# The second feed-forward's up products as seven products of halves

## The chip, the cores and the metric
The kernel runs on one core of one Trainium2 chip. The metric is the device time of one execution in microseconds; for the kernel before it is 1956.56 us, the median of 3 runs (1956.21 to 1960.05).

## What is computed
A diffusion backbone of two layers over 512 latent tokens (and 256 context tokens, which only the first layer still updates). Each layer has an attention part and a feed-forward part. The change concerns the feed-forward of the second layer, on the 512 latent tokens alone:

```python
def conv_ffn(h, w_up, conv_w, conv_b, w_down):
    u = h @ w_up                      # 512 x 1024 by 1024 x 5632
    n_tok = u.shape[1]
    pad = CONV_W // 2                 # CONV_W = 3
    up = jnp.pad(u, ((0, 0), (pad, pad), (0, 0)))
    u = sum(up[:, i:i + n_tok] * conv_w[i] for i in range(CONV_W)) + conv_b
    a, g = jnp.split(u, 2, axis=-1)   # 2816 columns each
    return (jax.nn.silu(g) * a) @ w_down

x = x + g2 * conv_ffn(modulate(x, g_ffn[l], sh2, s2), w_up[l], conv_w[l], conv_b[l], w_down[l])
```

All of it is float32.

## The kernel before
Activations are kept transposed: eight blocks of 128 features lie on the 128 partitions, tokens along the free dimension. TensorE multiplies in a reduced format (fp32r), so each operand is split in a high part (a rounded copy) and a low part (the rest), and a product is three matmuls: high by high, high by low, low by high (`mm3`, L254 to L257; the matmul itself is L252). `split` (L226) makes the two parts: the high part on ACT (L229) or POOL (L231), the low part on DVE (L237) or POOL (L239), as a subtraction of two SBUF tiles.

The normed tokens are 16 tiles: eight high (`self.hh`) and eight low (`self.hl`), in the group of buffers named E in the second layer; the running state x is eight tiles of the group F, and the feed-forward's hidden h goes to F too. `out_norm` computes the norm in two halves of 256 tokens: the last attention products and the residual update (L1335), squares on ACT (L530), sums by matmuls with a column of ones (L539), the root on POOL (L267, L269), its transpose on PE (the rows `pt<-ident,rr`, L261), scale and shift (L556, L557), and the split (high on POOL, low on DVE and POOL by turns).

`ffn` (L1465 on) goes over 22 pairs of up tiles: pair i is the 128 hidden columns i of the half a and the same of the half g (tile 22 + i). For a pair, `up_w` loads two weight tiles of 128 x 1024 (raw, buffers `fr`) and splits them (buffers `fu`; the second of pair 1 in `fd`), ACT the high and DVE the low part. `up_mm` makes eight steps of three matmuls with 512 columns for each tile into a PSUM tile `s`: 48 per pair. Pair 0 is done in two halves of 256 tokens, so that its first half needs only the first half of the norm. `up_tile` does the convolution: a scaled copy from PSUM on ACT (L1422) and taps on DVE that read PSUM (`tap`, L1440: two of 504 columns, two of 7). Then come silu on ACT (L1513), the product on DVE (L1514) and the split of h (high on POOL, low on DVE).

Pairs go in chunks of two. The down products of a chunk (`accumulate`: eight output blocks, 2 x 3 matmuls of 512 each, 48 per chunk, into PSUM tiles o, acc and pt, each followed by a residual update on DVE, L1335) run one chunk later, after the second pair's up products. Their weights come by `down_w` (buffers `fr` and `fd`). The last pair is finished in two halves by `last_part`.

The instruction streams of each engine are ordered by a scheduler that simulates the program on a timeline and takes what it holds to be ready; the order is then fixed. What can be taken early depends on buffers: the pool of the second layer's mixing part (its tiles u, s, raw among them) is closed before the pools of the feed-forward are opened, and where a new pool takes memory of an old one, its tiles wait for the old tiles' last readers. The pool for `fu` lies on the other side of the memory than that for `fr` and `fd`.

## Time and profile before

| | before |
|---|---|
| median of 3 runs | 1956.56 us |
| profiled execution | 1957.14 us |
| its span on the core | 1955.4 us |
| PE busy | 1857.2 us (95%) |
| DVE busy | 1189.5 us (61%) |
| ACT busy | 797.5 us (41%) |
| POOL busy | 748.4 us (38%) |
| second feed-forward | about 1581 us to the end of the span |

PE stands for TensorE's matmuls, PEld for its weight loads (which run beside them), DVE for VectorE, ACT for ScalarE, POOL for GpSimd. Busy time counts what an instruction takes on its engine. A row of a group gives line, engine, operation, output and inputs, shapes and count, then the busy time, the mean in ns, and the idle time before with what ended it. A row of a timeline gives start and duration in us, and how many instructions it sums. PEclk is the share of full clock that was granted to TensorE.

### The profile page before, as it was taken

To read this page: it belongs to the slowest core of one execution; us is meant where nothing else is said; L and a number is where in the kernel's file an instruction comes from. 1 tells how busy PE (TensorE), PEld (TensorE's weight loads), DVE (VectorE), ACT (ScalarE), POOL (GpSimd) and SP (SyncE) were. 2 spreads that over 40 slices of the span, in tenths; PEclk is the share of its full clock that TensorE was granted. 3 is DMA by queue.
4 is the path that set the end of the run, shared out by engine and by line. 5 is a ranking of instruction groups with operands and counts; after the bars stand their busy time and mean duration, and the time that the engine had idled before them with its cause. 6 is when DMAs were issued, how large, how long until landed. Compare 5 with 4: busy or idle time off the path is not lost.

```text
span 1955.4 us, 32438 instructions
## 1 busy us (share of the span) xinstructions
PE 1857.2 (95%) x12513; PEld 1613.9 (83%) x12513; DVE 1189.5 (61%) x2132; ACT 797.5 (41%) x1549; POOL 748.4 (38%) x1013
## 2 busy tenths in 40 slices
PE   5999999989999999999999999998989999999999
PEld 3778888878898788888888898887977788888888
DVE  5344566365467677865566575457356467666665
ACT  4336546375444222222222254655356453323332
POOL 4555363460045545668761047544362030000000
PEclk9999999899999999999999999999999999999999
DMA  9852333421213434254442124233431313333332
GB/s 315 293 166 53 99 82 84 130 94 48 79 42 113 112 98 137 80 171 138 122 134 69 60 71 113 53 96 100 107 105 58 91 50 104 93 96 93 97 97 76
DMA packets 177081, 206.19 MB, mean 105 GB/s; under 512 B 10848, under 2 KB 142784, under 8 KB 174880
## 3 DMA queue, kind: packets, MB, share of 16 engines
q1 hardware_dynamic: 175872, 201.96, 34.9%
q0 software_dynamic: 1056, 2.16, 0.4%
...
## 4 chain that ended last, share of the span: by engine, by line
PE 77%; DVE 7%; DMA 5%; POOL 5%; ACT 3%; issue 2%; SPq 1%; POOLq 0%; ACTq 0%; DVEq 0%
PE s L252 32%; PE acc L252 18%; PE pt L252 10%; PE o L252 6%; PE pt L261 5%; PE o L862 4%; DMA wr<-in_w_in 1%; DMA wr<-in_w_out 1%; POOL rr L269 1%; DVE fu L237 1%; POOL wh L239 1%; DVE m L816 1%; PE s L539 1%; DVE p L1440 1%; ACT p L819 1%
## 5 line engine op out<-in xcount | busy, mean ns | idle before, releaser
L252 PE MATMUL s<-F,fu 128*128 128x256 f32 (+1 forms) x2064 | 374.0, 336 | 0.3 <-DVE p L1440 0.3
L252 PEld LDWEIGHTS s<-F,fu 128*128 128x128 f32 x2064 | 314.1, 189 | 42.9 <-issue 0.4
L252 PE MATMUL s<-E,fu 128*128 128x512 f32 (+1 forms) x1056 | 239.7, 380 | 1.4 <-POOL E L231 1.2
L816 DVE TENSOR_REDUCE m<-s 128x1 f32<-128x768 f32 (+2 forms) x200 | 159.0, 804 | 116.8 <-PE s L252 115.5
L252 PEld LDWEIGHTS s<-E,fu 128*128 128x128 f32 x1056 | 192.7, 188 | 40.2 <-POOL E L231 1.4
L229 ACT ACTIVATE fu<-fr 128x1024 fp32r<-128x1024 f32 x90 | 95.1, 1060 | 282.0 <-PE s L252 175.9
L819 ACT ACTIVATE p<-s,m 128x768 f32<-128x768 f32 (+2 forms) x200 | 156.3, 783 | 90.9 <-DVE m L816 56.8
L1440 DVE SCALAR_TENSOR_TENSOR p<-s,cv,p 128x7 f32<-128x7 f32 (+4 forms) x428 | 184.4, 471 | 10.0 <-ACT p L1448 3.7
L237 DVE TENSOR_TENSOR fu<-fr,fu 128x1024 fp32r<-128x1024 f32 x90 | 121.6, 1351 | 82.1 <-ACT fu L229 81.7
L252 PE MATMUL acc<-wh,E 128*128 128x256 f32 (+2 forms) x1164 | 164.1, 294 | 6.3 <-ACT tq L1289 2.2
L252 PE MATMUL acc<-wh,F 128*128 128x256 f32 (+2 forms) x1188 | 160.4, 286 | 5.9 <-DVE wh L237 2.3
L252 PEld LDWEIGHTS acc<-wh,E 128*128 128x128 f32 x1164 | 151.8, 200 | 11.7 <-ACT tq L1289 2.7
L252 PEld LDWEIGHTS acc<-wh,F 128*128 128x128 f32 x1188 | 147.5, 190 | 11.5 <-DVE wh L237 3.1
L261 PE MATMUL pt<-ident,p 128*128 128x128 f32 x771 | 122.1, 280 | 18.8 <-DMA p<-in_crow 9.8
L842 ACT ACTIVATE pw<-pt 128x512 f32<-128x512 f32 x192 | 112.7, 597 | 66.3 <-PE pt L261 65.7
L231 POOL TENSOR_SCALAR F<-p 128x512 fp32r<-128x512 f32 x21 | 13.1, 622 | 313.4 <-DVE p L1514 313.4
L419 POOL TENSOR_TENSOR mx<-mx,wm 128x384 f32<-128x384 f32 x112 | 120.1, 1090 | 2.8 <-ACT mx L414 1.5
L261 PEld LDWEIGHTS pt<-ident,p 128*128 128x128 f32 x771 | 90.0, 143 | 31.7 <-DMA p<-in_crow 10.2
L229 ACT ACTIVATE fd<-fr 128x1024 fp32r<-128x1024 f32 x42 | 44.1, 1058 | 151.2 <-PE pt L252 96.8
L269 POOL TENSOR_TENSOR rr<-ms,mhalf 128x4 f32<-128x4 f32 (+4 forms) x75 | 102.3, 1364 | 3.6
L231 POOL TENSOR_SCALAR E<-p 128x768 fp32r<-128x768 f32 x21 | 19.2, 913 | 208.4 <-DVE p L1514 204.6
L418 POOL TENSOR_SCALAR wm<-wm,sc 128x384 f32<-128x384 f32 x112 | 96.5, 872 | 5.9 <-DVE mx L416 3.4
...
## 6 DMA issues: line engine op xcount, KB each, us to landing
...
```

What stands on the lines that cost most here:

```text
L229: nc.scalar.activation(hi, src, AF.Copy)
L237: nc.vector.tensor_tensor(lo, src, hi.bitcast(F32), op=ALU.subtract)
L252: self.nc.tensor.matmul(out, lhsT=lhsT, rhs=rhs, start=start, stop=stop)
L261: self.nc.tensor.transpose(out, in_, self.ident[:k, :k])
L269: nc.gpsimd.tensor_tensor(r, m, self.mhalf[:, :n], op=ALU.pow)
L418: self.behind("pool", nc.gpsimd.tensor_scalar(src, src, s, 0.0, op0=ALU.mult, op1=ALU.add))
L419: nc.gpsimd.tensor_tensor(dst, dst, src, op=ALU.add)
L816: nc.vector.tensor_reduce(out=m, in_=sv, axis=ax, op=ALU.max, negate=True)
L819: nc.scalar.activation(pv, sv, AF.Exp, bias=m, accum_out=it.l[hi_][:, h:h + 1])
L842: self.nc.scalar.activation(w, pt, AF.Copy)
L862: self.nc.tensor.matmul(it.o[r, :P], lhsT=v, rhs=it.w[b][:, a, h], start=(n == 0 and a == 0), stop=(n == it.nb - 1 and a == 1), tile_posit ...
L1440: self.nc.vector.scalar_tensor_tensor(y[:, dst:dst + n], in0=src, scalar=w, in1=y[:, dst:dst + n], op0=ALU.mult, op1=ALU.add)
```

## The change
From the fourth pair on (`SEVEN = 3`), in the second layer only, the up products of a pair are made by a scheme of Strassen's in the form with 15 additions. The two weight tiles of the pair, each in two halves of 512 input features by 128 columns, form a 2 x 2 block; so do the tokens (first and last four feature blocks, first and second 256 tokens). Instead of eight block products (48 matmuls of 512 columns) there are seven (84 matmuls of 256 columns), of the blocks themselves (a11, a22, a12) and of sums of blocks (s1 to s4).

What comes with it: the sums of the tokens, once, during pairs 0 and 1 (`token_sums`: 40 additions of 128 x 256 on POOL, then splits on ACT and DVE, kept in unused thirds of E, ab and mx, with the unused thirds of F as scratch); the sums of the weights per pair on POOL (`weight_sums`, four of 128 x 512, in place in the raw tiles); splits by halves, those of s1, s3 and s4 with the low part on POOL (`up_half`); the low part of the down weights on POOL too; and the sums of the seven products into two SBUF tiles `ca` and `cg` (`seven`: two copies on ACT and seven additions of 256 columns on DVE, with one operand in PSUM). The seven products of 256 columns are placed in eight half banks of two PSUM tiles. The convolution then reads SBUF: `conv_sums` copies 7 columns to each end and taps 511 columns at once. The high part of h moves from POOL to ACT. Buffers: `fr` 2 to 3, `p3` 4 of 768 to 6 of 528 columns, `fu` 6 of 1024 to 14 of 512. In the last chunk the down weights are loaded after the up products, in halves. The line numbers shift: the matmul L252 is L254 after, L229/L231/L237/L239 are L231/L233/L239/L241, L1335 is L1337, the tap L1440 is L1562, L1514 is L1669; L1441 is a weight sum, L1422 and L1423 are token sums, L1486 is an addition of products.

```diff
-    FFN = (dict(fd=4, p3=4, fr=2, fu=6), dict(fr=2, p3=4, fd=4))
-    UPW = dict(fu=6)
+    FFN = (dict(fd=4, p3=4, fr=2, fu=6), dict(fr=3, p3=6, fd=4))
+    UPW = dict(fu=14)
+    SEVEN = 3
...
+    def up_half(self, src, lo_eng="dve"):
+        hi, lo = self.t("fu", [P, 512], F32R), self.t("fu", [P, 512], F32R)
+        self.split(src, hi, lo, "act", lo_eng)
+        return hi, lo
...
+    def token_sums(self, k, pairs, tmp):
+        nc = self.nc
+        sub = lambda o, a, b: nc.gpsimd.tensor_tensor(o, a, b, op=ALU.subtract)
+        add = lambda o, a, b: nc.gpsimd.tensor_tensor(o, a, b, op=ALU.add)
+        blk = lambda kk, j: [t[kk][:, j * 256:(j + 1) * 256].bitcast(F32) for t in (self.hh, self.hl)]
+        b11, b12, b21, b22 = blk(k, 0), blk(k, 1), blk(4 + k, 0), blk(4 + k, 1)
+        t1, t2, t3, t4, d = tmp
+        for o, a, b in ((t1, b12, b11), (t3, b22, b12)):
+            sub(o, a[0], b[0])
+            sub(d, a[1], b[1])
+            add(o, o, d)
+        for o, a, b in ((t2, b22, t1), (t4, b21, t2)):
+            sub(o, a[0], b)
+            add(o, o, a[1])
+        for o, (hi, lo) in zip((t1, t2, t3, t4), pairs):
+            self.split(o, hi, lo, "act", "dve")
+        return pairs
+    def weight_sums(self, l, i):
+        nc = self.nc
+        g = lambda o, a, b, op: nc.gpsimd.tensor_tensor(o, a, b, op=op)
+        a, c = self.t("fr", [P, 1024]), self.t("fr", [P, 1024])
+        self.up_load(l, i, a)
+        self.up_load(l, NFF + i, c)
+        a11, a12, a21, a22 = a[:, :512], a[:, 512:], c[:, :512], c[:, 512:]
+        w = {}
+        def s1():
+            g(a22, a21, a22, ALU.add)
+            g(a21, a11, a21, ALU.subtract)
+            g(a11, a22, a11, ALU.subtract)
+            w["s1"] = self.up_half(a22, "pool")
+        def s4():
+            g(a12, a12, a11, ALU.subtract)
+            w["s4"] = self.up_half(a12, "pool")
+        one = lambda n, src, eng="dve": lambda: w.__setitem__(n, self.up_half(src, eng))
+        return w, [one("a11", a11), one("a22", a22), s1, one("s2", a11), one("s3", a21, "pool"), one("a12", a12), s4]
+    def seven(self, l, i, w, T, ps, nxt):
+        nc = self.nc
+        half = lambda kk, j: lambda k: [t[kk + k][:, j * 256:(j + 1) * 256] for t in (self.hh, self.hl)]
+        nxt = list(nxt)
+        def prod(name, b):
+            n = self.nprod % 8
+            self.nprod += 1
+            s = ps[n % 4 // 2][:, n % 2 * 512 + n // 4 * 256:][:, :256]
+            hi, lo = w[name]
+            for k in range(4):
+                c = slice(k * P, (k + 1) * P)
+                first, last = self.mm3(s, hi[:, c], lo[:, c], *b(k), k == 0, k == 3)
+                if k == 0 and n % 4 in self.bank:
+                    info = mybir.DependencyInfo(mybir.DependencyClass.NoSync, mybir.DependencyReason.DATA)
+                    self.tc.add_manual_dep(first.ins, self.bank[n % 4].ins.name, info, reason="bank")
+            self.bank[n % 4] = last
+            if nxt:
+                nxt.pop(0)()
+            return s
+        ca, cg = (self.t("p3", [P, 528]) for _ in range(2))
+        lo, hi = slice(8, 264), slice(264, 520)
+        add = lambda o, a, b: nc.vector.tensor_tensor(o, a, b, op=ALU.add)
+        p = prod("a11", half(0, 0))
+        nc.scalar.activation(ca[:, hi], p, AF.Copy)
+        nc.scalar.activation(ca[:, lo], p, AF.Copy)
+        p4 = prod("a22", lambda k: T[k][3])
+        p5 = prod("s1", lambda k: T[k][0])
+        add(ca[:, hi], ca[:, hi], prod("s2", lambda k: T[k][1]))
+        add(cg[:, lo], ca[:, hi], prod("s3", lambda k: T[k][2]))
+        add(cg[:, hi], cg[:, lo], p5)
+        add(ca[:, hi], ca[:, hi], p5)
+        add(ca[:, lo], ca[:, lo], prod("a12", half(4, 0)))
+        add(cg[:, lo], cg[:, lo], p4)
+        add(ca[:, hi], ca[:, hi], prod("s4", half(4, 1)))
+        return ca, cg
+    def conv_sums(self, l, c, ti):
+        nc = self.nc
+        cv = lambda a: self.cv[:, a, l, ti:ti + 1]
+        y = self.t("p3", [P, 528])
+        nc.scalar.activation(c[:, 1:8], c[:, 512:519], AF.Copy)
+        nc.scalar.activation(c[:, 520:527], c[:, 9:16], AF.Copy)
+        nc.scalar.activation(y[:, :TL], c[:, 8:520], AF.Identity, scale=cv(1), bias=cv(3))
+        self.tap(y, 1, c[:, 1:512], 511, cv(0))
+        self.tap(y, 0, c[:, 16:527], 511, cv(2))
+        return y
...
+    def down_w(self, l, k, tag, lo_eng="dve"):
+        self.split(raw, hi, lo, "act", lo_eng)
...
+        self.bank, self.nprod, sums = {}, 0, []
+        if l + 1 == DEPTH:
+            more = [self.big(t, F32R) for t in ["ab"] * 5 + ["mx"]]
+            third = lambda t: t[:, 512:768]
+            more = [t[:, o:o + 256] for t in more for o in (0, 256, 512)]
+            pairs = [(third(a), third(b)) for a, b in zip(self.hh, self.hl)] + [(more[2 * n], more[2 * n + 1]) for n in range(8)]
+            tmp = [third(t) for t in self.x]
+        seven = self.SEVEN if l + 1 == DEPTH else NFF
+        if seven == NFF:
+            prep = lambda i: ups.__setitem__(i, (self.up_w(l, i), self.up_w(l, NFF + i, "fd" if i == 1 else "fu")))
+        else:
+            prep = lambda i: ups.__setitem__(i, (self.up_halves(l, i), self.up_w(l, NFF + i, "fd") if i == 1 else self.up_halves(l, NFF + i)))
         prep(0)
         for ci, ch in enumerate(chunks):
             acts, wts = [], []
             for n_, i in enumerate(ch):
-                if i + 1 < NFF:
+                steps = []
+                if i + 1 < seven:
                     prep(i + 1)
+                elif i + 1 < NFF:
+                    ups[i + 1], steps = self.weight_sums(l, i + 1)
                 ws = ups.pop(i)
+                N = sum(n for _, n in segs)
+                if i + 1 == seven:
+                    for f in steps[:3]:
+                        f()
...
+                elif i >= seven:
+                    if i == seven:
+                        banks = [self.psum("s") for _ in range(2)]
+                    cs = self.seven(l, i, ws, sums, banks, steps)
+                    if i < NFF - 1:
+                        ya, yg = (self.conv_sums(l, c, j) for c, j in zip(cs, (i, NFF + i)))
+                    else:
+                        ys = [self.up_y(l) for _ in cs]
+                        hi, lo = self.big("h2", F32R), self.big("h2", F32R)
+                        for c0, n, _ in cols_last:
+                            self.last_part(l, [(c[:, 8:520], j) for c, j in zip(cs, (i, NFF + i))], ys, hi, lo, c0, n)
...
+                        if i + 1 == seven:
+                            for f in steps[3:5] if j == i else steps[5:]:
+                                f()
                         ys.append(self.up_tile(l, s, j, segs)[0])
...
+                    if l + 1 < DEPTH:
+                        self.split(yg[:, :N], hi[:, :N], lo[:, :N], "pool", mark=True)
+                    else:
+                        self.split(yg[:, :N], hi[:, :N], lo[:, :N], "act")
                 acts.append((hi, lo))
+                if seven < NFF and i < 2:
+                    sums += [self.token_sums(k, pairs[4 * k:4 * k + 4], tmp[k % 2 * 3:k % 2 * 3 + 5]) for k in (2 * i, 2 * i + 1)]
...
-                wts.append(self.down_w(l, i, "fu" if last else "fd"))
+                if not last:
+                    wts.append(self.down_w(l, i, "fd", "pool" if i >= seven else "dve"))
+                elif seven == NFF:
+                    wts.append(self.down_w(l, i, "fu"))
+                elif n_:
+                    wts += [self.down_halves(l, j) for j in ch]
```

The order of the instructions up to the end of the second layer's attention stays. On PE, around the start of the second feed-forward (s: up products, or the sums for the norm, whose rows read `ones`; pt: the last attention products; the last number in a name tells buffers apart), there stands before:

```order
L252 MATMUL pt_18123<-F_17865,ab_17878 128x256
L252 MATMUL s_18280<-E_17882,fu_18257 128x256
L252 MATMUL s_18280<-E_17890,fu_18257 128x256
L252 MATMUL s_18280<-E_17882,fu_18258 128x256
L252 MATMUL s_18280<-E_17883,fu_18257 128x256
L539 MATMUL s_18024<-ones,raw_18076 128x1 x2
L539 MATMUL s_18024<-ones,raw_18096 128x1 x2
L539 MATMUL s_18024<-ones,raw_18116 128x1 x2
L252 MATMUL s_18280<-E_17891,fu_18257 128x256
L252 MATMUL s_18280<-E_17883,fu_18258 128x256
```

and after:

```order
L254 MATMUL pt_18123<-F_17865,ab_17878 128x256
L541 MATMUL s_18024<-ones,raw_18076 128x1 x2
L541 MATMUL s_18024<-ones,raw_18096 128x1 x2
L541 MATMUL s_18024<-ones,raw_18116 128x1 x2
L541 MATMUL s_18024<-ones,raw_18136 128x1 x2
L541 MATMUL s_18024<-ones,raw_18156 128x1 x2
L541 MATMUL s_18024<-ones,raw_18176 128x1 x2
L263 MATMUL pt_18191<-ident,rr_18189 128x128 x2
L254 MATMUL s_18298<-E_17882,fu_18264 128x256
L254 MATMUL s_18298<-E_17890,fu_18264 128x256
```

The first up products stood ahead of and between the sums of the second half of the norm; they stand behind these and behind the transpose of rr. On ACT the first split of up weights stood before the last splits of the attention's output weights (wh, ab); it stands behind the last scale and shift of the norm (L559), with splits of token sums between the weight halves that follow.

On POOL, the splits of the second half of the normed tokens (E from u and s; eight blocks), before:

```order
L231 TENSOR_SCALAR E_17882<-u_18194 128x256
L231 TENSOR_SCALAR E_17883<-s_3808_18199 128x256
L231 TENSOR_SCALAR E_17884<-u_18204 128x256
L231 TENSOR_SCALAR E_17885<-u_18209 128x256
L239 TENSOR_TENSOR E_17893<-u_18209,E_17885 128x256
L231 TENSOR_SCALAR E_17886<-s_3811_18214 128x256
L231 TENSOR_SCALAR E_17887<-u_18219 128x256
L231 TENSOR_SCALAR E_17888<-u_18224 128x256
L231 TENSOR_SCALAR E_17889<-s_3814_18229 128x256
L239 TENSOR_TENSOR E_17897<-s_3814_18229,E_17889 128x256
```

and after, where L1422 and L1423 make token sums into thirds of F:

```order
L233 TENSOR_SCALAR E_17882<-u_18194 128x256
L1422 TENSOR_TENSOR F_17412<-E_17882 128x256
L233 TENSOR_SCALAR E_17883<-s_3808_18199 128x256
L1422 TENSOR_TENSOR F_17416<-E_17890 128x256
L233 TENSOR_SCALAR E_17884<-u_18204 128x256
L233 TENSOR_SCALAR E_17885<-u_18209 128x256
L1422 TENSOR_TENSOR F_17419<-E_17891 128x256
L1423 TENSOR_TENSOR F_17412<-F_17412,F_17416 128x256
L241 TENSOR_TENSOR E_17893<-u_18209,E_17885 128x256
L233 TENSOR_SCALAR E_17886<-s_3811_18214 128x256
L233 TENSOR_SCALAR E_17887<-u_18219 128x256
L1422 TENSOR_TENSOR F_17414<-E_17886,E_17882 128x256
```

The token sums stand between the splits; of the latter seven of eight have been reached in the rows shown.

In a later pair, POOL has before one split of h per pair, here behind the last split of tokens:

```order
L239 TENSOR_TENSOR E_17897<-s_3814_18229,E_17889 128x256
L231 TENSOR_SCALAR F_18392<-p_3830_18384 128x512
L231 TENSOR_SCALAR F_18478<-p_3845_18470 128x512
L231 TENSOR_SCALAR F_18564<-p_3860_18556 128x512
L231 TENSOR_SCALAR F_18714<-p_3883_18706 128x512
```

and after the sums of weights (L1441) and the low halves (L241), here for a pair and a half:

```order
L1441 TENSOR_TENSOR fr_20258<-fr_20259,fr_20258 128x512
L241 TENSOR_TENSOR fu_20314<-fr_20259,fu_20313 128x512
L241 TENSOR_TENSOR fu_20347<-fr_20259,fu_20346 128x512
L1441 TENSOR_TENSOR fr_20258<-fr_20258 128x512
L241 TENSOR_TENSOR fu_20385<-fr_20258,fu_20384 128x512
L1441 TENSOR_TENSOR fr_20414<-fr_20414 128x512
L1441 TENSOR_TENSOR fr_20414<-fr_20413,fr_20414 128x512
L241 TENSOR_TENSOR fu_20469<-fr_20414,fu_20468 128x512
L1441 TENSOR_TENSOR fr_20413<-fr_20414,fr_20413 128x512
```

The split of h is gone from POOL, and seven operations of 512 per pair are there, with one of 1024 for the down weights that is not in this piece. DVE has in a later pair before (low weights, taps, product, low part of h):

```order
L237 TENSOR_TENSOR fu_19906<-fr_19904,fu_19905 128x1024
L1440 SCALAR_TENSOR_TENSOR p_4073_19886<-s_19861,cv,p_4073_19886 128x504
L1440 SCALAR_TENSOR_TENSOR p_4073_19886<-s_19861,cv,p_4073_19886 128x7
L1440 SCALAR_TENSOR_TENSOR p_4073_19886<-s_19861,cv,p_4073_19886 128x504
L1440 SCALAR_TENSOR_TENSOR p_4073_19886<-s_19861,cv,p_4073_19886 128x7
L1514 TENSOR_TENSOR p_4073_19886<-p_4073_19886,p_4071_19855 128x512
L237 TENSOR_TENSOR F_19895<-p_4073_19886,F_19894 128x512
```

and after (additions of products L1486, taps L1562):

```order
L1486 TENSOR_TENSOR p_4137_20263<-p_4136_20262,s_18764 128x256
L1486 TENSOR_TENSOR p_4137_20263<-p_4137_20263,s_18765 128x256
L1486 TENSOR_TENSOR p_4136_20262<-p_4136_20262,s_18765 128x256
L239 TENSOR_TENSOR F_20185<-p_4120_20176,F_20184 128x512
L1486 TENSOR_TENSOR p_4136_20262<-p_4136_20262,s_18764 128x256
L1486 TENSOR_TENSOR p_4137_20263<-p_4137_20263,s_18764 128x256
L1486 TENSOR_TENSOR p_4136_20262<-p_4136_20262,s_18765 128x256
L1562 SCALAR_TENSOR_TENSOR p_4152_20389<-p_4136_20262,cv,p_4152_20389 128x511
L1562 SCALAR_TENSOR_TENSOR p_4153_20395<-p_4137_20263,cv,p_4153_20395 128x511
L1562 SCALAR_TENSOR_TENSOR p_4152_20389<-p_4136_20262,cv,p_4152_20389 128x511
L239 TENSOR_TENSOR fu_20330<-fr_20258,fu_20329 128x512
L1562 SCALAR_TENSOR_TENSOR p_4153_20395<-p_4137_20263,cv,p_4153_20395 128x511
```

The first tap stands right behind the last addition.

## Rows read from the trace of the kernel before

**Rows 1.** The page: span and busy time of each engine.
```profile
span 1955.4 us, 32438 instructions
...
PE 1857.2 (95%) x12513; PEld 1613.9 (83%) x12513; DVE 1189.5 (61%) x2132; ACT 797.5 (41%) x1549; POOL 748.4 (38%) x1013
```

**Rows 2.** The page: shares of the chain of waits, by engine.
```profile
PE 77%; DVE 7%; DMA 5%; POOL 5%; ACT 3%; issue 2%; SPq 1%; POOLq 0%; ACTq 0%; DVEq 0%
```

**Rows 3.** Window: us, busy of PE, PEld, DVE, ACT, POOL, PEclk, DMA share, GB/s.
```profile
1741.70:1774.90 33.20, 33.20 (x146) 27.20 (x145) 22.16 (x34) 10.30 (x12) 1.24 (x2) 1.00 0.30 95
```

**Rows 4.** Timeline of PE there: start, duration, operation, count of runs of 512 columns.
```profile
1709.42 1.57 PE L252 MATMUL pt<-F,fd 128*128 128x512 f32 x6
1710.83 6.52 PE L252 MATMUL s<-E,fu 128*128 128x512 f32 x28
```

**Rows 5.** Timeline of PE, runs of 256 columns (first layer).
```profile
1004.23 0.86 PE L252 MATMUL acc<-E,fd 128*128 128x256 f32 x6
1004.93 0.87 PE L252 MATMUL pt<-E,fd 128*128 128x256 f32 x6
```

**Rows 6.** DVE groups by shape, 1490 to 1956 us: busy, mean ns, idle before.
```profile
L1440 DVE SCALAR_TENSOR_TENSOR p<-s,cv,p 128x504 f32<-128x504 f32 x80 | 59.0, 738 | 1.7 <-ACT p L1422 0.7
L237 DVE TENSOR_TENSOR fu<-fr,fu 128x1024 fp32r<-128x1024 f32 x45 | 55.1, 1225 | 36.4 <-ACT fu L229 36.1
L1335 DVE SCALAR_TENSOR_TENSOR F<-pt,mT,F 128x512 f32<-128x512 f32 x38 | 27.6, 746 | 12.7 <-PE pt L252 12.7
...
L1440 DVE SCALAR_TENSOR_TENSOR p<-s,cv,p 128x7 f32<-128x7 f32 x84 | 18.1, 216 | 0.0
...
L1514 DVE TENSOR_TENSOR p<-p,p 128x512 f32<-128x512 f32 x21 | 14.5, 692 | 14.4 <-ACT p L1513 14.4
...
L556 DVE TENSOR_TENSOR u<-F,pt 128x256 f32<-128x256 f32 x10 | 4.1, 414 | 4.6 <-PE pt L261 3.4 <-POOL E L239 1.0
```

**Rows 7.** POOL groups by shape, whole span.
```profile
L239 POOL TENSOR_TENSOR wh<-wr,wh 128x512 fp32r<-128x512 f32 x32 | 42.8, 1339 | 2.1
...
L537 POOL TENSOR_TENSOR raw<-raw,raw 128x256 f32<-128x256 f32 x12 | 9.2, 769 | 17.9 <-ACT raw L530 17.8
```

**Rows 8.** DVE groups by shape, 700 to 1150 us (first feed-forward).
```profile
L237 DVE TENSOR_TENSOR fu<-fr,fu 128x1024 fp32r<-128x1024 f32 x33 | 50.8, 1540 | 33.1 <-ACT fu L229 33.1
L1440 DVE SCALAR_TENSOR_TENSOR p<-s,cv,p 128x504 f32<-128x504 f32 x64 | 47.1, 735 | 0.6
```

**Rows 9.** Timeline of DVE, 233 to 236 us.
```profile
234.05 1.02 DVE L827 SCALAR_TENSOR_TENSOR p<-p,c,p 128x768 f32<-128x768 f32 x1
```

**Rows 10.** Timeline of DVE, 300 to 306 us.
```profile
302.59 2.15 DVE L827 SCALAR_TENSOR_TENSOR p<-p,c,p 128x768 f32<-128x768 f32 x1
```

**Rows 11.** Timeline of POOL, 300 to 306 us.
```profile
302.63 1.29 POOL L239 TENSOR_TENSOR wh<-wr,wh 128x512 fp32r<-128x512 f32 x1
```

**Rows 12.** Timeline of PE at the start of the second feed-forward.
```profile
1581.34 0.64 PE L252 MATMUL s<-E,fu 128*128 128x256 f32 x4
...
1586.53 3.50 PE L252 MATMUL s<-E,fu 128*128 128x256 f32 x26
1589.87 0.38 PE L261 MATMUL pt<-ident,rr 128*128 128x128 f32 x2
...
1608.91 3.36 PE L252 MATMUL s<-E,fu 128*128 128x512 f32 x14
```

**Rows 13.** Timeline of POOL there: splits of the normed tokens.
```profile
1591.49 0.41 POOL L231 TENSOR_SCALAR E<-u 128x256 fp32r<-128x256 f32 x1 [2.50 <-ACT u L557]
...
1594.87 0.74 POOL L239 TENSOR_TENSOR E<-u,E 128x256 fp32r<-128x256 f32 x1
...
1598.56 0.74 POOL L239 TENSOR_TENSOR E<-s,E 128x256 fp32r<-128x256 f32 x1
```

**Rows 14.** ACT groups by shape, 1490 to 1956 us.
```profile
L229 ACT ACTIVATE wh<-wr 128x512 fp32r<-128x512 f32 x7 | 4.3, 632 | 3.4 <-DMA wr<-in_w_out 2.7 <-PE o L252 0.6
```

More of the change, by code (lines that the diff above doesn't have):

```diff
@@ L251, in mm @@
     def mm(self, out, lhsT, rhs, start, stop):
-        self.nc.tensor.matmul(out, lhsT=lhsT, rhs=rhs, start=start, stop=stop)
+        return self.nc.tensor.matmul(out, lhsT=lhsT, rhs=rhs, start=start, stop=stop)
     def mm3(self, out, lh, ll, rh, rl, start, stop):
-        self.mm(out, lh, rh, start, False)
+        first = self.mm(out, lh, rh, start, False)
         self.mm(out, lh, rl, False, False)
-        self.mm(out, ll, rh, False, stop)
+        return first, self.mm(out, ll, rh, False, stop)
     def tr(self, out, in_):
@@ L1410, in up_tile, with up_y @@
+    def up_y(self, l):
+        return self.t("p3", [P, T if l + 1 < DEPTH else 528])
     def up_tile(self, l, s, ti, segs):
```

26 lines of the change are left out of this document (16 added, 10 removed).

## Prediction

> **What bounds the kernel now.** I read the page first, then the chain, then windows of the stage that changes, then timelines and groups by shape for the prices. The profiled execution took 1957.14 us, 1955.4 us of it span; the median of the runs shown is 1956.56, so what I add to the one holds for the other within 0.6 us. PE is busy for 95% of the span [rows 1] and 77% of the chain of waits is PE [rows 2]. In the second layer's feed-forward this is sharper: a window of 33.2 us, in which two pairs of tiles pass (144 products of 512 columns), shows PE busy for all 33.20, DVE for 22.16, ACT for 10.30 and POOL for 1.24, at a granted clock of 1.00 [rows 3]. So a pair costs 33.2 / 2 = 16.6 us, a product of 512 columns 33.2 / 144 = 0.2306 us, and nothing but PE's own work sets the pace. Fewer PE columns can pay here as long as the other engines stay under the new pace. POOL, idle now, and DVE, two thirds full, are the ones to check.
>
> **The change, term 1: PE's work in the 19 later pairs.** Removed are 48 products of 512 columns per pair, added are 84 of 256 (seven products, four blocks, three hi/lo parts). The 24 down products of a pair stay. The price of a narrow product is read where a run of six is followed at once by the next: 1004.93 - 1004.23 = 0.70 us for six, 0.117 each [rows 5]. The same reading for wide ones is 1710.83 - 1709.42 = 1.41 for six, 0.235 each [rows 4]. Half the columns cost half the time. A pair becomes 84 x 0.118 + 24 x 0.2306 = 15.45 us instead of 16.6: 1.15 less, 22 us over 19 pairs, if PE still paces.
>
> **Term 2: what the other engines need per pair.** POOL gets four weight sums of 512, three lo halves of 512 and one lo of 1024, which I count as nine pieces of 512. One such piece took 1.29 us [rows 11] (1.339 in the mean [rows 7]): 9 x 1.29 = 11.6 us, where it had 0.6.
> DVE loses the lo of two up tiles and of the down tile (1.225 each [rows 6]) and four taps of 7 (0.216); it gains four lo halves of 512 and seven adds of 256 with one PSUM operand (0.414, as the add from PSUM in the norm [rows 6]). Its list is then: ten instructions with both inputs in SBUF, namely four weight lo, the lo of h, the product (0.692 each, as the product [rows 6]) and four taps (0.738), 7.1 us; seven adds, 2.9; four residual updates of 0.746, 3.0. Together 13.0. The same count for before gives 11.85 where the window shows 22.16 / 2 = 11.1, since successive instructions overlap by some 0.05 us; with 21 instructions I take 12.0. Before, the taps read PSUM; now they read SBUF, and the order has a tap straight behind the last add, although it first needs ACT's wrap copies and its scaled copy: about 1.3 us of DVE waiting (two small ACT operations and one of 512, from the 0.632 of a 512 copy [rows 14]). Behind that tap stand the other taps, the product, the lo of h and the weight lo of the next pair, which PE's next products wait for. That makes 13.3, under 15.45.
> What the old trace shows only elsewhere is how DVE and POOL get on. The same DVE instruction of 768 on SBUF took 1.02 us alone [rows 9] and 2.15 beside a POOL lo of 512 [rows 10, 11]; it ended 0.82 us after POOL's, so it had been held until some 0.2 us before that. In the first feed-forward, where POOL is working, DVE's lo of 1024 takes 1.540 in the mean against 1.225, but the taps that read PSUM keep 0.735 [rows 6, 8]. So only the ten SBUF-SBUF instructions suffer, and the change gives DVE more of them (the taps) and POOL 11 us more of work to collide with.
> Price of it, by two ways. By DVE: POOL works 11.6 of some 16.7 us, so 0.69 of the ten meet it, and each waits for the half of 1.29 left over less 0.2, that is 0.45: 3.1 us; 13.3 + 3.1 = 16.4. By the two together, if they exclude each other: 7.1 + 11.6 = 18.7, less 0.2 at each of ten hand-overs = 16.7. I take 16.7 per pair, the second, since POOL's lo and sums are on the way of the next products and DVE's adds free the PSUM slots: +0.1 per pair, +2 us in 19. The bounds are 15.45 (-22) and 18.7 (+40).
>
> **Term 3: the start of the feed-forward.** Before, PE fills the wait for the second half of the norm with products of the first half: the first at 1581.34, 44 of them ahead of the transposes of rr at 1589.87; the third pair begins at 1608.91 [rows 12], and the last lo of the tokens ends at 1599.30 [rows 13]. After, all 96 narrow products of pair 0 stand behind those transposes, because the weights' halves lie in memory that the norm's tile u still holds: ACT's first split of weights waits for the last u. The transposes come earlier by some 3 us (no products ahead of them, no weight splits on ACT), so that POOL's first hi split starts near 1588.5 in place of 1591.49. But POOL's row of splits now has token sums in between: up to the seventh block six splits at some 0.45 and five TENSOR_TENSOR of 256 at 0.77 [rows 7, 13], 6.5 us, so 1595.0. Then lo and ACT's split of 0.632: the first twelve products can start at about 1596.7. The next weight half stands on ACT behind a split of a token sum, which waits for five more POOL operations and a hi: 4.3 us later, ready at about 1600.4. From there 84 x 0.118 = 9.9 and pair 1 with 48 x 0.2306 = 11.1 end at 1621.4, against 1608.91: +12.5, and +1 for DVE, which has the token lo and the weights' lo at once. I take +13.5. The lower bound is no second hold (1596.7 + 11.3 + 11.1 = 1619.1, +10), the upper +19 with the other token sums (7 x 0.77) also ahead. Nothing hides this: PE has no other work in that place.
>
> **Term 4: the end.** The last pair's combining adds come before its taps, and the last down weights are loaded later, as halves: two or three adds of 0.414 and an ACT copy on the path, +2 (0 to 4). The ACT additions else (splits of h and of halves, 0.632 each [rows 14]) lie beside PE: ACT has 10.3 of 33.2 busy [rows 3] and would get some 5 per pair more.
>
> **Sum.** +2 + 13.5 + 2 = 17.5: 1957.1 + 17.5 = 1974.6, so 1975.
>
> **Rivals.** *A, PE keeps the pace.* If DVE and POOL fall out of each other's way (waits below 2 us a pair), a pair takes 15.45 to 15.9 and the 19 give back 20: -20 + 12 + 1 = -7, 1950. For it: DVE has 13.3 without waits, and weight halves may be split ahead of their use while a buffer is free. Against: rows 8 and 10. It decides from 15.9 per pair down, where the gain exceeds the start's loss.
> *B, the two engines exclude each other without overlap.* 18.7 per pair less a little, say 18.2: +30 + 13.5 + 2, 2003. For it: rows 9 to 11; against: 0.2 us of overlap in each. [...]
> *C, narrow products cost more than half.* The break-even is 48 x 0.2306 / 84 = 0.132 us. At 0.147 (a quarter more) a pair is 17.9, +25 + 13.5 + 2: 1997. Against it stands 0.117 in rows 5. [...]
> **How the numbers follow.** The forecast (16.2 to 17.6 per pair, 1960 to 1992) has 0.49, A 0.26, B 0.21, C 0.04. The range leaves a tenth out on each side: 1947 takes most of A, 2006 the middle of B. 0.2% of this time is 3.9 us, about what a measurement can tell from none. A is faster in 0.20, level in 0.05 and slower in 0.01; the forecast's lower edge (a start of +10 and 16.0 a pair, -11 + 10 + 1) adds 0.04 level. Faster 0.20, same 0.09, slower 0.71.
>
> **What would show it.** Term 1: the cadence of the 256 products near 0.118. Term 2: windows of two pairs near 33.4 us, PE busy below 95% of them, DVE lo, taps and product means of 0.9 to 1.1 instead of 0.69 and 0.74, adds and residuals unchanged, POOL busy 70% or more. Term 3: the first product of the feed-forward after the rr transposes, near 1597, and the third pair's start near 1622. Wrong it would be if two pairs take below 32 us, or if the third pair starts before 1615.

## The result, and the profile after

The changed kernel takes 2029.02 us (median of 4 runs, 2024.28 to 2031.11) against 1956.38: ratio 1.0367, 95% interval 1.0349 to 1.0386, slower. Forecast were 1975 and a range up to 2006: the direction was right, the size not. The page's totals, which answer to [rows 1, 2]:

```profile
span 2027.0 us, 34478 instructions
...
PE 1861.1 (92%) x13197; PEld 1642.5 (81%) x13197; DVE 1283.9 (63%) x2235; ACT 876.2 (43%) x1798; POOL 1002.2 (49%) x1184
```
```profile
PE 63%; DVE 12%; POOL 8%; DMA 7%; ACT 5%; issue 4%; SPq 1%; POOLq 0%; ACTq 0%; DVEq 0%
```

PE falls from 77% to 63% of the chain of waits; DVE, POOL, ACT and DMA gain. To see where the 71.6 us of span lie I count from the last copy of attention on ACT (u from o), since all before it is the same program, and read four later marks: the first product on PE of the third pair (pair 2, the last that is made the old way), the silu of pair 4, that of pair 18, and the end. Timeline of ACT, before and after (start, duration):

```profile
1550.83 0.28 ACT L867 ACTIVATE u<-o 128x128 f32<-128x128 f32 x1 [1.81 <-PE o L862]
...
1662.45 0.63 ACT L1513 ACTIVATE p<-p 128x512 f32<-128x512 f32 x1 [4.23 <-DVE p L1440]
...
1893.45 0.63 ACT L1513 ACTIVATE p<-p 128x512 f32<-128x512 f32 x1 [4.23 <-DVE p L1440]
```
```profile
1555.72 0.28 ACT L869 ACTIVATE u<-o 128x128 f32<-128x128 f32 x1 [1.81 <-PE o L864]
...
1700.11 0.62 ACT L1668 ACTIVATE p<-p 128x512 f32<-128x512 f32 x1
...
1960.73 0.62 ACT L1668 ACTIVATE p<-p 128x512 f32<-128x512 f32 x1
```

With the third pair at 1608.91 [rows 12] and at 1629.08 (below): the unchanged part ended 4.9 us later in this execution (1555.7 - 1550.8); up to the third pair +15.3 (73.4 against 58.1); from there to pair 4, which I call the passage, +17.5 (71.0 against 53.5); the 14 pairs from 4 to 18 +29.6 (260.6 against 231.0, that is 18.62 us a pair against 16.50); the rest +4.3. These make 71.6. Pairs 3 and 4, the first two by the scheme, lie inside the passage, and pairs 19 to 21 inside the rest.

The start, timeline of PE (after), and windows of it (us, then busy time of PE, PEld, DVE, ACT and POOL, PEclk, DMA share, GB/s):

```profile
1590.66 0.69 PE L263 MATMUL pt<-ident,rr 128*128 128x128 f32 x2 [2.50 <-POOL rr L271]
1604.29 13.88 PE L254 MATMUL s<-E,fu 128*128 128x256 f32 x96 [12.94 <-ACT fu L231]
1618.01 5.64 PE L254 MATMUL pt<-E,fu 128*128 128x512 f32 x24
...
1629.08 1.29 PE L254 MATMUL s<-E,fu 128*128 128x512 f32 x5
```
```profile
1591.40:1604.20 12.80, 0.00 (x0) 0.00 (x0) 7.75 (x15) 5.60 (x11) 11.92 (x20) 0.50 0.00 1
1604.30:1611.10 6.80, 6.75 (x39) 6.46 (x40) 6.80 (x8) 3.98 (x9) 5.64 (x6) 0.69 0.34 87
```

PE stands for 12.9 us while POOL is busy for 11.9 of 12.8 with splits and token sums. The granted clock stood at 0.50 in this gap and at 0.69 in the mean over the next 6.8 us, and only 39 narrow products fit into these.

The later pairs, windows of the 14 pairs before and after:

```profile
1662.50:1893.50 231.00, 231.00 (x1010) 189.22 (x1009) 155.09 (x238) 72.11 (x85) 8.70 (x14) 1.00 0.32 96
```
```profile
1700.10:1960.70 260.60, 230.65 (x1512) 207.99 (x1511) 209.45 (x293) 123.90 (x252) 172.75 (x112) 0.99 0.28 84
```

No engine is full any more: PE shows gaps, DVE has 80%, POOL 66%. The price of products in this stretch, on the timeline of PE, and DVE's and POOL's groups by shape (busy, mean ns, idle before), which answer to [rows 4 to 7]:

```profile
1719.77 1.59 PE L254 MATMUL s<-E,fu 128*128 128x256 f32 x12
1721.20 1.55 PE L254 MATMUL o<-F,fd 128*128 128x512 f32 x6
1722.59 1.59 PE L254 MATMUL s<-E,fu 128*128 128x256 f32 x12
```
```profile
L1562 DVE SCALAR_TENSOR_TENSOR p<-p,cv,p 128x511 f32<-128x511 f32 x56 | 54.3, 1020 | 12.3 <-ACT p L1508 12.3
L239 DVE TENSOR_TENSOR fu<-fr,fu 128x512 fp32r<-128x512 f32 x55 | 53.7, 990 | 6.7 <-ACT fu L231 6.4
L1486 DVE TENSOR_TENSOR p<-p,s 128x256 f32<-128x256 f32 x97 | 37.6, 413 | 15.6 <-PE s L254 15.4
L1337 DVE SCALAR_TENSOR_TENSOR F<-pt,mT,F 128x512 f32<-128x512 f32 x28 | 20.5, 745 | 6.3 <-PE pt L254 6.2
L1669 DVE TENSOR_TENSOR p<-p,p 128x512 f32<-128x512 f32 x14 | 16.5, 1176 | 2.4 <-ACT p L1668 2.4
L239 DVE TENSOR_TENSOR F<-p,F 128x512 fp32r<-128x512 f32 x14 | 15.2, 1083 | 3.8 <-ACT F L231 3.8
```
```profile
L241 POOL TENSOR_TENSOR fu<-fr,fu 128x512 fp32r<-128x512 f32 x42 | 60.9, 1452 | 29.0 <-ACT fu L231 29.0
```

1721.20 - 1719.77 = 1.43 us for twelve narrow products is 0.119, and 1.39 for six wide ones 0.232: PE's own work is 84 x 0.119 + 24 x 0.232 = 15.6 us a pair, close to the 15.45 forecast. The pair takes 3.0 us more than that; in 2.1 of these ((260.6 - 230.65) / 14) the window has PE idle, and in the rest PE counts as busy without keeping this cadence. Instructions with both inputs in SBUF are stretched (0.990, 1.020, 1.083, 1.176 against 0.69 and 0.74), those that read PSUM are not (0.413, 0.745). What PE waits for, and a piece of the chain of waits (start, us, what):

```profile
PE s L254 <- DVE p L1486: 18.0, 18, 1.9
PE o L254 <- ACT F L231: 7.6, 5, 2.4
PE s L254 <- ACT p L1489: 2.6, 5, 0.8
PE s L254 <- ACT fu L231: 1.2, 2, 0.6
```
```profile
1774.34 2.45 DVE p L1669
1776.78 0.34 DVE p L1486
...
1777.17 1.71 PE s L254 x12
...
1778.90 0.43 DVE p L1486
...
1779.47 0.81 ACT p L1508
...
1780.30 4.17 DVE p L1562 x4
```

PE waits most for the additions that free PSUM slots (18.0 us), then for the split of h (`F`, 7.6), hardly for weights. An addition stands on DVE behind the product of the pair before, here 2.45 us long, and behind taps, 4.17 for four.

### The profile page after: what moved, and what is told of

Same layout as the page of the kernel before. It is cut to its first block, busy times and chain, and to the rows that moved or that the text cites. A ratio compares the mean times of both kernels' runs of the same rounds, so it can differ in the third digit from the quotient of the medians.

```text
span 2027.0 us, 34478 instructions
## 1 busy us (share of the span) xinstructions
PE 1861.1 (92%) x13197; PEld 1642.5 (81%) x13197; DVE 1283.9 (63%) x2235; ACT 876.2 (43%) x1798; POOL 1002.2 (49%) x1184
## 4 chain that ended last, share of the span: by engine, by line
PE 63%; DVE 12%; POOL 8%; DMA 7%; ACT 5%; issue 4%; SPq 1%; POOLq 0%; ACTq 0%; DVEq 0%
PE s L254 23%; PE acc L254 17%; PE pt L254 8%; PE o L254 5%; PE pt L263 5%; PE o L864 4%; DVE p L1562 3%; DVE fu L239 2%; DMA wr<-in_w_in 2%; DMA fr<-in_w_up 1%; DMA wr<-in_w_out 1%; POOL fr L1441 1%; POOL F L1422 1%; DMA F<-ab 1%; DVE p L1669 1%
## 5 line engine op out<-in xcount | busy, mean ns | idle before, releaser
L254 PE MATMUL s<-F,fu 128*128 128x256 f32 (+1 forms) x2064 | 373.7, 335 | 0.3 <-DVE p L1562 0.3
L254 PEld LDWEIGHTS s<-F,fu 128*128 128x128 f32 x2064 | 313.9, 189 | 42.8 <-issue 0.4
L231 ACT ACTIVATE fu<-fr 128x512 fp32r<-128x512 f32 (+1 forms) x192 | 134.8, 726 | 275.0 <-PE s L254 149.6
L254 PE MATMUL s<-E,fu 128*128 128x256 f32 (+1 forms) x1284 | 186.1, 292 | 43.7 <-DVE p L1486 23.6
L254 PEld LDWEIGHTS s<-E,fu 128*128 128x128 f32 x1284 | 171.1, 194 | 57.8 <-DVE p L1486 20.8
L239 DVE TENSOR_TENSOR fu<-fr,fu 128x512 fp32r<-128x512 f32 (+1 forms) x133 | 152.4, 1154 | 56.6 <-ACT fu L231 56.1
L254 PE MATMUL acc<-wh,F 128*128 128x256 f32 (+2 forms) x1188 | 159.9, 285 | 6.0 <-DVE wh L239 2.3
L254 PE MATMUL acc<-wh,E 128*128 128x256 f32 (+2 forms) x1164 | 157.6, 286 | 6.4 <-ACT tq L1291 2.5
L254 PEld LDWEIGHTS acc<-wh,F 128*128 128x128 f32 x1188 | 147.1, 189 | 12.0 <-DVE wh L239 3.1
L254 PEld LDWEIGHTS acc<-wh,E 128*128 128x128 f32 x1164 | 145.0, 191 | 11.9 <-ACT tq L1291 3.0
L844 ACT ACTIVATE pw<-pt 128x512 f32<-128x512 f32 x192 | 112.6, 596 | 65.2 <-PE pt L263 64.7
L263 PE MATMUL pt<-ident,p 128*128 128x128 f32 x771 | 122.6, 280 | 18.2 <-DMA p<-in_crow 10.2
L233 POOL TENSOR_SCALAR E<-p 128x768 fp32r<-128x768 f32 x21 | 19.1, 911 | 208.0 <-DVE p L1669 190.6
L1562 DVE SCALAR_TENSOR_TENSOR p<-s,cv,p 128x504 f32<-128x504 f32 (+4 forms) x272 | 117.5, 472 | 5.8 <-ACT p L1544 2.6
L241 POOL TENSOR_TENSOR fu<-fr,fu 128x512 fp32r<-128x512 f32 x59 | 85.2, 1447 | 40.9 <-ACT fu L231 40.9
L873 POOL TENSOR_SCALAR rx<-r 128x128 f32<-128x128 f32 x60 | 20.0, 334 | 167.5 <-DVE r L833 126.4
```

The costliest lines, as they stand in the source:

```text
L231: nc.scalar.activation(hi, src, AF.Copy)
L239: nc.vector.tensor_tensor(lo, src, hi.bitcast(F32), op=ALU.subtract)
L241: nc.gpsimd.tensor_tensor(lo, src, hi.bitcast(F32), op=ALU.subtract)
L254: return self.nc.tensor.matmul(out, lhsT=lhsT, rhs=rhs, start=start, stop=stop)
L263: self.nc.tensor.transpose(out, in_, self.ident[:k, :k])
L844: self.nc.scalar.activation(w, pt, AF.Copy)
```

## Experiments

All against before in the same session; marks counted as above (third pair minus before; passage; us a pair between the silu of pairs 4 and 18; before: 0, 53.5, 16.50). Each mark is read from one profiled execution. The order of the instructions on the engines is fixed anew for every edited kernel, so a kernel can differ from another by more than the edit shown.

| kernel | median us | ratio, 95% interval | third pair | passage | a pair |
|---|---|---|---|---|---|
| changed kernel | 2029.0 | 1.0367 [1.0349, 1.0386] | +15.3 | 71.0 | 18.62 |
| fu12 | 2022.6 | 1.0349 [1.0330, 1.0369] | +10.2 | 72.5 | 18.85 |
| late | 2026.4 | 1.0358 [1.0339, 1.0377] | +14.2 | 71.1 | 18.79 |
| fu12_late | 2028.0 | 1.0374 [1.0357, 1.0390] | +7.3 | 74.2 | 19.13 |
| tok_off | 2012.0 | 1.0287 [1.0269, 1.0304] | +10.0 | 64.0 | 18.69 |
| tok_off12 | 2003.0 | 1.0220 [1.0176, 1.0265] | +0.4 | 60.3 | 18.99 |
| seven13 | 1999.6 | 1.0223 [1.0197, 1.0249] | +14.2 | 54.0 | 16.65, then 20.52 |
| pool_off | 1992.8 | 1.0195 [1.0179, 1.0210] | +16.0 | 63.7 | 17.26 |
| dlo_off | 2041.9 | 1.0442 [1.0426, 1.0458] | +14.5 | 77.0 | 20.06 |
| both_off | 1983.7 | 1.0139 [1.0118, 1.0160] | +14.3 | 67.1 | 16.64 |
| taps_short | 1996.0 | 1.0190 [1.0136, 1.0244] | +14.3 | 69.0 | 17.14 |
| tt_dummy | 2010.2 | 1.0257 [1.0192, 1.0321] | +6.3 | 82.7 | 17.98 |
| ms_dummy | 1979.4 | 1.0107 [1.0060, 1.0154] | +6.4 | 70.4 | 16.79 |
| pool_taps | 1985.6 | 1.0132 [1.0087, 1.0178] | +15.0 | 64.7 | 16.81 |
| fr4 | 2033.2 | 1.0398 [1.0342, 1.0455] | +20.1 | 68.9 | 19.29 |
| all_off12 | 1967.8 | 1.0060 [1.0034, 1.0085] | -0.7 | 61.4 | 17.02 |

**The start: fu12, late, fu12_late, tok_off, tok_off12.**

```diff
-    UPW = dict(fu=14)
+    UPW = dict(fu=12)                      # fu12
-                if seven < NFF and i < 2:
+                if seven < NFF and 1 <= i < 3: # late; k in (2 * i - 2, 2 * i - 1)
+        return [[t[kk][:, j * 256:(j + 1) * 256] for t in (self.hh, self.hl)] for kk in (k, 4 + k) for j in (0, 1)]   # tok_off
```

> The buffers fu are 12 in place of 14, so that their pool takes the same memory as before the change and no longer overlaps the tile u of the norm; all else as in the changed kernel. Theory M (the overlap of memory holds back the first products of the second feed-forward): the first product comes well before 1600 us, the third pair starts near 1612 instead of 1629, and the time falls by some 15 us to 2014. Theory S (the token sums that POOL makes between the splits of the norm hold them back): products still start near 1604, time 2025 to 2031. Fewer buffers could cost later pairs a little in both.

> The token sums are given out one pair later (during pairs 1 and 2 in place of 0 and 1); buffers as in the changed kernel. Theory S: POOL's splits of the norm are free of them, the tokens are ready near 1596 to 1599, products start near 1597 instead of 1604, and the time falls by 7 to 10 us to about 2020, unless the sums then hold up pair 3. Theory M: as the weights' memory is still held, at most 3 us are won.

> Both edits: 12 buffers fu and token sums one pair later. If both things are needed at once (the start is held by whichever comes last), only this one lets first products run ahead of the rr transposes as before the change, third pair near 1610, and gives back the whole 20 us of the start: about 2010. If the start were no part of the loss: 2029. What stays above 1956 is then the later pairs: 16 pairs with about 1.9 us each and the passage at pairs 2 and 3.

> The token sums (40 additions on POOL, 16 splits on ACT and 16 on DVE during pairs 0 and 1) are not made; the products read blocks of the tokens in their place. Counted from the end of attention, the changed kernel loses 15 us up to the third pair and a further 17 between there and pair 4. Theory T (both come from the token sums, in front of the splits and as a backlog on DVE): the third pair starts 10 us earlier or more and the passage costs under 5: about 25 us less, 2002. Theory W (the passage is the weights' work that begins with pair 3, and the start is held by memory): under 8 us less.

> Token sums not made, and 12 buffers fu. If the start is held by whichever of the two comes last, it goes altogether here: third pair 58 to 60 us after the end of attention as before the change, where each alone left 68. The passage to pair 4 keeps what pair 3's weights cost, 8 to 10 us. Total about 10 us under the kernel without token sums: near 2002. If token sums alone count: no change against it, 2012.

In fu12 the first product comes at 1583.41, the third pair still at +10.2, so neither theory had it whole; with late alone next to nothing is won, as theory M had it; without token sums alone +10.0, and 2012.0 in all lies between T and W. Only tok_off12 has the start of before: first product at 1579.34, its third pair at 1606.82, 58.5 us after the end of attention:

```profile
1606.82 11.05 PE L254 MATMUL s<-E,fu 128*128 128x512 f32 x48
```

So memory and token sums hold the start side by side: either alone costs 10, both together 15.3, less than their sum and more than the later of the two. Giving the sums out later moves their work to the next pairs (fu12_late: third pair still +7.3, passage 74.2) and wins nothing in all. My expectation for fu12_late (2010) was wrong: the third pair's products still wait for DVE's taps, which stand behind splits of token sums there.

```profile
1621.17 12.54 PE L254 MATMUL s<-E,fu 128*128 128x512 f32 x48 [5.04 <-DVE p L1562]
```

**POOL's work: pool_off.** Weight sums on 32 columns, low parts of s1, s3, s4 and of the down weights left out.

```diff
-        g = lambda o, a, b, op: nc.gpsimd.tensor_tensor(o, a, b, op=op)
+        g = lambda o, a, b, op: nc.gpsimd.tensor_tensor(o[:, :32], a[:, :32], b[:, :32], op=op)
+        if lo_eng == "pool":
+            self.nc.scalar.activation(hi, src, AF.Copy)
+            return hi, hi
...                             # the same in down_w
```

> From pair 3 on POOL's work is left out: weight sums are made on 32 columns in place of 512, and the low parts of s1, s3, s4 and of the down weights are not made (PE reads the high part twice, so its work is the same). Theory P (POOL's work, by excluding DVE and by its own time, sets the pace): a pair falls from 18.6 us to 15.5 to 16.2, DVE's low parts and taps return to 0.69 and 0.74 us; 18 pairs give back 43 to 55 us: about 1980. Theory D (DVE's own added list with its waits for ACT's copies and for PSUM sets the pace): low parts and taps get faster but a pair stays above 17.3, time above 2005.

17.26 lies between the two: without POOL's work a pair is 1.4 us shorter and the passage 7, but a pair is still 1.7 above PE's own 15.6, and 1.1 of that is idle PE ((241.6 - 226.29) / 14 in the window of its 14 pairs).

**Where DVE's work stands: dlo_off, taps_short, both_off, pool_taps.**

```diff
-        one = lambda n, src, eng="dve": ...
+        one = lambda n, src, eng="none": ...          # dlo_off: no low part, return hi, hi
-        self.tap(y, 1, c[:, 1:512], 511, cv(0))
-        self.tap(y, 0, c[:, 16:527], 511, cv(2))
+        self.tap(y, 1, c[:, 1:65], 64, cv(0))         # taps_short
+        self.tap(y, 0, c[:, 16:80], 64, cv(2))
```

> POOL works in full; on DVE the four low parts of weights per later pair (a11, a22, s2, a12) are not made, PE reads the high part in their place. In the changed kernel a later pair takes 18.6 us, of which PE idles 3.0. Theory D (PE idles because DVE comes late with the additions that free the PSUM slots; DVE had 16.2 us of work per pair, 4 x 0.99 less now): a pair falls to 16 to 16.8, about 14 x 2 = 28 us less in the steady part. Theory P (POOL's chain of sums and low parts holds the weights back, whatever DVE does): a pair stays at 18 or more, 5 us less at most.

> The four taps of a later pair are made on 64 columns in place of 511, all else in full (leaves out most of the convolution's neighbours). It takes about as much work from DVE (4 x 0.8) as leaving out four low parts of weights did, which made the kernel slower. Theory H (what counts is not DVE's sum but what stands ahead of the next additions in its fixed order: last addition, ACT's copies, taps, silu, product, only then the additions that free PSUM slots): a pair falls from 18.6 us to 17 or less, time to about 2000. Theory P (POOL's chain of weights): a pair stays at 18 or more, 2020 or more.

taps_short leaves out less of DVE's work, 4 x (1.020 - 0.444) = 2.3 us a pair against 4 x 0.990 = 4.0 in dlo_off. Yet dlo_off got slower, against theory D and further than P had it: DVE's groups there show the taps longer still (1.465 us against 1.020), PE waits longer for additions (32.8 us in 240 against 18.0 in 260), and its 14 pairs have a lower granted clock, 0.93 against 0.99 (dlo_off in the first three rows, taps_short in the last):

```profile
L1565 DVE SCALAR_TENSOR_TENSOR p<-p,cv,p 128x511 f32<-128x511 f32 x48 | 67.7, 1465 | 11.0 <-ACT p L1511 11.0
```
```profile
1696.60:1977.40 280.80, 239.12 (x1512) 218.28 (x1512) 183.59 (x239) 123.21 (x251) 176.08 (x112) 0.93 0.26 79
```
```profile
PE s L254 <- DVE p L1489: 32.8, 15, 4.4
```
```profile
L1562 DVE SCALAR_TENSOR_TENSOR p<-p,cv,p 128x64 f32<-128x64 f32 x56 | 23.8, 444 | 19.6 <-ACT p L1508 18.6
```

At the lower clock of 0.93 the same 1512 products keep PE busy for 239.1 us against 230.7, 0.6 of the 1.4 us that a pair is longer than in the changed kernel. Why the taps take longer in dlo_off was not taken apart. taps_short, with POOL's work in full, saves 1.5 a pair. What DVE has to do in all does not set the pace. That it is what stands between the last addition of a pair and the first ones of the next fits the chain above and both kernels, but it is argued, since the order changed with the edits.

> Both: POOL's work of later pairs left out (sums on 32 columns, no low parts of s1, s3, s4 and down weights) and DVE's four low parts left out. With POOL's alone left out a pair took 17.26 us, with PE's own work 84 x 0.1196 + 24 x 0.233 = 15.64. Theory D: the 1.6 us left are DVE's; a pair falls to 15.7 to 16.0. Theory S (the 1.6 are the order: PE's fixed order, ACT's copies of the first product, the waits from add to add in eight PSUM slots): a pair stays above 16.6 although both engines have time.

> POOL's work of later pairs left out as in the kernel with 17.26 us a pair (idle additions none), and the four taps on 64 columns besides. Theory H (the chain behind the last addition delays the next pair's additions, which free PSUM slots): a pair falls to 15.7 to 16.3, PE idles under 0.6 us of it. Theory S (PE's fixed order and ACT's copies of the first product): it stays at 16.8 or more, as with the low parts left out besides (16.64).

Without POOL's work neither the low parts nor the taps matter that much (17.26 to 16.64 and to 16.81, where D expected 16.0 and H 16.3 or less), and theory S is left, by exclusion. In pool_taps PE waits most for ACT's second copy of the first product; in both_off it waits 7.2 us for additions and 0.9 for that copy, at about the same pace. Waits of PE in pool_taps:

```profile
PE s L254 <- ACT p L1492: 7.8, 6, 1.9
PE s L254 <- DVE p L1489: 3.1, 6, 0.5
```

**The longer DVE instructions by themselves: tt_dummy and ms_dummy,** both as pool_off, with 12 fu and idle work on POOL.

```diff
+    def dummy(self):
+        self.nc.gpsimd.tensor_tensor(self.dm[0], self.dm[1], self.dm[1], op=ALU.subtract)    # in tt_dummy
+        [self.nc.gpsimd.memset(self.dm[0], 0.0) for _ in range(3)]                           # in ms_dummy
...                             # called nine times for each pair
```

> As the kernel with POOL's work of later pairs left out (17.26 us a pair), but with nine idle additions of 512 columns per pair put on POOL, which read and write two tiles of their own; nothing waits for their results. 12 buffers fu. Theory L (exclusion between POOL and DVE on SBUF): DVE's low parts, taps and products go back to 0.95 to 1.15 us and a pair to 18 or more. Theory C (it was POOL's results that came late): DVE's instructions may lengthen, but a pair stays near 17.3.

> The same, but each idle addition is replaced by three fills of 512 columns with a constant, about as long together (0.20 us for 128 columns in the trace of before), which read nothing. Theory L: DVE's instructions keep 0.69 to 0.75 us, a pair stays near 17.3 though POOL is as busy as with the additions. If POOL's time alone were the cause, it would take as long as with the additions.

DVE's and POOL's groups, tt_dummy first, then ms_dummy, and the windows of their 14 pairs:

```profile
L239 DVE TENSOR_TENSOR fu<-fr,fu 128x512 fp32r<-128x512 f32 x50 | 48.9, 979 | 2.6 <-ACT fu L231 1.5 <-PE s L254 0.6
L1577 DVE SCALAR_TENSOR_TENSOR p<-p,cv,p 128x511 f32<-128x511 f32 x48 | 46.1, 983 | 13.9 <-ACT p L1517 13.8
```
```profile
1695.40:1947.20 251.80, 229.44 (x1514) 207.65 (x1514) 195.62 (x295) 124.99 (x255) 173.58 (x183) 0.99 0.29 88
```
```profile
L1577 DVE SCALAR_TENSOR_TENSOR p<-p,cv,p 128x511 f32<-128x511 f32 x50 | 36.1, 747 | 12.4 <-ACT p L1517 12.4
L239 DVE TENSOR_TENSOR fu<-fr,fu 128x512 fp32r<-128x512 f32 x52 | 35.9, 691 | 9.0 <-ACT fu L231 8.6
```
```profile
1687.50:1922.50 235.00, 224.54 (x1514) 204.50 (x1513) 169.13 (x294) 123.18 (x253) 207.31 (x422) 1.00 0.31 95
```

POOL is busier with the fills (207.3 of 235.0 us against 173.6 of 251.8), yet DVE keeps its 0.69 and 0.75 and a pair takes 16.79 instead of 17.98. So it is not POOL's busy time that goes with DVE's longer instructions here: beside POOL's additions, which read SBUF, DVE's low parts and taps take 0.979 and 0.983 us, beside its fills, which read nothing, 0.691 and 0.747. The 1.2 us a pair are the price of that only about, since DVE's order is not quite the same in the two. (Both have a longer passage than pool_off; the idle work begins with pair 3's weights.)

What the order may do shows in ms_dummy against pool_off. POOL does more, DVE's instructions are as long, and a pair is still 0.5 us shorter (16.79 against 17.26). In one of two pairs the scheduler put the next pair's first addition ahead of the last tap; in pool_off it stands behind all four and a low part. DVE in pool_off, then in ms_dummy:

```profile
1787.65 2.78 DVE L1569 SCALAR_TENSOR_TENSOR p<-p,cv,p 128x511 f32<-128x511 f32 x4 [1.10 <-ACT p L1511]
1790.35 0.69 DVE L239 TENSOR_TENSOR fu<-fr,fu 128x512 fp32r<-128x512 f32 x1
1790.95 0.42 DVE L1489 TENSOR_TENSOR p<-p,s 128x256 f32<-128x256 f32 x1
```
```profile
1785.45 1.41 DVE L1577 SCALAR_TENSOR_TENSOR p<-p,cv,p 128x511 f32<-128x511 f32 x2
1786.78 0.41 DVE L1495 TENSOR_TENSOR p<-p,s 128x256 f32<-128x256 f32 x1
1787.11 0.74 DVE L1577 SCALAR_TENSOR_TENSOR p<-p,cv,p 128x511 f32<-128x511 f32 x1
```

ms_dummy has 12 buffers fu besides, and no kernel was made in which the order alone changed.

**Raw buffers: fr4.**

```diff
-    dict(fr=3, p3=6, fd=4)
+    dict(fr=4, p3=6, fd=4)      # and UPW = dict(fu=12)
```

> 12 buffers fu and four raw weight buffers fr in place of three. Theory R (POOL's in-place sums wait for the raw tiles, which come late since only three fit): a pair falls by 0.5 us or more against the kernel with 12 fu and three fr (18.85), total 2012 or less. Theory L/H (exclusion on SBUF, and DVE's order): a pair stays at 18.5 to 19, total 2016 to 2026.

Theory R falls: a fourth raw buffer does not help. A pair takes 19.29, longer than in fu12 (18.85) and than L/H had it; why it is longer was not looked into.

**The whole: seven13 and all_off12.**

```diff
-    SEVEN = 3
+    SEVEN = 13                  # seven13; all_off12: fu12, tok_off, both_off together
```

> The scheme starts at pair 13 in place of 3, all else the same, so that ten pairs are done as before (16.5 us) and nine by the scheme. If the loss is a start (15 us), a passage (17 us) and 2.1 us for each pair after it: 10 x 2.1 = 21 us less, 2008, and the passage moves to pairs 12 to 14. If the passage is a backlog of the token sums, which lie ten pairs back by then, it goes too: about 1991.

> What the scheme could give at most in this frame: token sums not made, sums of weights on 32 columns, no low parts in later pairs but h's, 12 buffers fu so that first products run during the norm. PE's work is that of the changed kernel. If the frame is sound: start within 3 us of before, a pair at 15.7 to 16.2 against 16.5, about 1945 to 1952. If the order on PE (products that wait for additions and for ACT's copies) costs as in the runs so far, a pair is 16.6 and the total is above 1960: then no mending of POOL or DVE makes the scheme pay here.

seven13, at 1999.6 between its two expectations, keeps the pairs of before at 16.65 and loses 24.8 us over the six pairs 13 to 18 (20.52 against 16.39): six times 2.1 and 12 of passage, though the token sums lie ten pairs back. The changed kernel's passage counted in the same way, without twice 2.1 for pairs 3 and 4, is 17.5 - 4.2 = 13.3. So by seven13 the change-over costs nearly all of it, and the token sums cost next to nothing of it by themselves: seven13 makes them in its stretch up to pair 4 too, which takes 54.0 against 53.5. Yet tok_off's passage is 7.0 shorter. The token sums seem to cost that only where the change-over meets them, and how the 13.3 divide stays open. all_off12, without token sums, weight sums and low parts, but with the additions of products, ACT's copies and the high parts, has the start of before and still takes 17.02 a pair: slower than before by 0.3 to 0.9%, as its second expectation had it (above 1960). No variant beat the kernel before.

## Why the prediction missed

- *Term 1, PE's work* (-22): right. The narrow product costs 0.119 us and the wide one 0.232, and rival C, which needed more than 0.132, is out. Over the 14 pairs PE's work fell by 14 x (16.5 - 15.6) = 12.6 us, while the time rose by 29.6.
- *Term 2, "I take 16.7 per pair"*: the step that failed; measured 18.62, +2.1 a pair in place of +0.1. Its parts were sound: DVE's waits were put at 3.1 us a pair and are 4 x (0.990 - 0.692) + 4 x (1.020 - 0.738) + (1.176 - 0.692) + (1.083 - 0.692) = 3.2. The error was to take the largest sum over an engine, or over two taken to exclude each other, as the pace. The runs show a chain across PE, DVE and ACT in fixed orders, with no engine full: without POOL's work a pair is still 1.7 above PE's own 15.6; DVE's longer instructions beside POOL's additions add about 1.2 (17.98 in tt_dummy against 16.79 in ms_dummy); another 0.9 lie between tt_dummy and fu12, which has as many buffers (17.98, 18.85), perhaps POOL's results being waited for, which was not tested by itself. These shares do not add up exactly, since kernels whose orders differ lie up to 0.5 apart without any other cause found (ms_dummy, pool_off). The taps' wait for ACT, 1.3 us a pair in my sum for DVE, was 0.9 (12.3 us in 14 pairs) and stands on that chain.
- *A term that was missing*: the passage, +17.5. I had no term for it; the +1 for DVE belonged to the start. Some 4 of it are pairs 3 and 4 at the pace of the later ones, so 13 stand beside term 2. They come with the change-over to the scheme (12 in seven13) and shrink by 7 without token sums (tok_off) and as much without POOL's work of later pairs (pool_off); what takes the time within the change-over was not taken apart.
- *Term 3, the start* (+13.5): +15.3, within its bounds of +10 to +19, in part by luck. Memory and token sums both hold it (tok_off12), as argued. But the products began 2.7 us later than my 1596.7 (1604.3, less the 4.9 of the unchanged part), ran on without the second hold that I had counted, and lost about as much again, by an estimate, at the lower clock behind the gap (0.69 over the first 6.8 us): the 96 took 1618.01 - 1604.29 = 13.7 us, where 96 x 0.119 is 11.4.
- *Term 4, the end* (+2): right within its 0 to 4. Of the +4.3 from pair 18 on, +1.2 lie up to the silu of pair 20, and +3.1 behind it (35.0 us to the end against 31.9).
- *The rest*: 4.9 us of the span lie in the unchanged program ahead and belong to the one execution.
- *Rivals*: A is refuted (18.62, and 17.26 in pool_off, even without POOL's work). B had the right time for a pair (18.2 to 18.7) but for a reason that is only part of it: dlo_off lowers the two engines' joint work and takes 20.06. With the passage's 13 on top, B's 2003 would have been about 2016.
